# Regrouping the batches of a rope kernel: two single batches at each end, six even pairs between

## The chip, the cores and the metric

The kernel runs on one core of one Trainium2 chip. Times are device microseconds of an execution; the profile's span (first to last instruction) is 1.4 to 1.6 us shorter. Executions fall into a fast and a slow state (before: 161.58 to 161.92 us in five of six runs, 169.21 in one). A run counts as slow when it is over 1.5% above the fastest of the same kernel. Engines are DVE (VectorE), POOL (GpSimd), PE (TensorE), ACT (ScalarE) and SP (SyncE); transfers run on 16 DMA engines (in the packet records of the first profile, of before, 16 or 17 packets are in flight at every half microsecond from 158.0 to 162.5).

## The reference

```python
# x (16, 512, 1024) f32, 16 heads of 64; cos, sin (512, 32)
x = x.reshape(batch, seq, num_heads, 64)
x1, x2 = x[..., :32], x[..., 32:]
rotated = concatenate([x1 * cos - x2 * sin, x1 * sin + x2 * cos], axis=-1)   # f32
```

In and out are 33.55 MB each, and every element is read once and written once.

## The kernel before

A "row" below is one 128 x 1024 piece of work. DVE multiplies it by cos into PSUM (t1), POOL or DVE multiplies the swapped halves by sin into SBUF (t2), and either DVE adds the two, or PE adds t2 onto t1 and ACT copies the sum out. The sum overwrites x in its buffer and is stored from there. A batch alone puts 4 rows on a partition (16 KB packets), a pair of batches 8 rows (32 KB packets); in the packet records of the first profile each transfer has 128 of them.

```python
tiles = [(0, R1)] + [(b, R2) for b in range(1, batch - 1, 2)] + [(batch - 1, R1)]   # R1 = 4, R2 = 8
REGIONS = 5                                              # buffers of 8 rows, used in turn
loads = [(t, r, n) for t, (_, whole) in enumerate(tiles)
         for n in (R1 if t == 1 else whole,) for r in range(0, whole, n)]   # the first pair in two halves
PE2 = [tiles[t][1] == R2 and r in (1, 3, 6) for t, r in rows]    # rows that PE adds
V2 = [tiles[t][1] == R2 and r == V_ROW for t, r in rows]         # rows that DVE multiplies by sin
...
def on_sync(sp):                                         # all loads
    for c, (t, r, n) in enumerate(loads):
        if t >= REGIONS:
            sp.wait_ge(sem_out[t - REGIONS], 16)         # the store that frees the buffer
        sp.dma_start(in_sbuf(t, r, n), in_dram(x1, x2, t, r, n)).then_inc(sem_in[c], 16)
        ...                                              # with the first load, those of cos and sin
...
def on_scalar(ae):                                       # copies of PE's rows, and all stores
    for u in range(NU):
        ...
        if r == tiles[t][1] - 1:
            wait_added(ae, u)
            ae.dma_start(in_dram(o1, o2, t, 0, r + 1), in_sbuf(t, 0, r + 1)).then_inc(...)
...
for u in range(NU + LEAD):                               # DVE; LEAD = 1
    if u < NU: mul(u)                                    # waits for the load of row u
    if u >= LEAD and not PE2[u - LEAD]: comb(u - LEAD)   # the addition of the row before
```

The addition of a transfer's last row comes after the multiply of the next transfer's first row, so a store also waits for the next load.

## Time and profile before

| | before |
|---|---|
| time, median of 6 runs | 161.70 us |
| fast runs | 161.58 to 161.92 us |
| slow run | 169.21 us |
| first profile (slow) | 169.03 us, span 167.5 us |
| POOL, DVE busy in it | 134.2 us, 131.0 us |
| bytes moved | 67.26 MB |

How to read it: POOL and DVE are busy about 80% of a span in which the DMA engines are busy 94%.

### The profile page before, as it was taken

Reading aid. Unit: us, or ns where it says so; the run is one execution under the profiler, and the core shown is the slowest. Engines: PE = TensorE matmul, PEld = TensorE weight load, DVE = VectorE, ACT = ScalarE, POOL = GpSimd, SP = SyncE. Lnnn points to the kernel's source line nnn. Section 1 sums busy time; section 2 is a strip of 40 time slices with the busy share of each in tenths; the row PEclk is TensorE's granted clock in tenths of the full one; section 3 lists DMA queues with packets and bytes.
Section 4 is the critical chain, followed back from the end, with each engine's and each line's share of the span. In section 5 each row is a group of like instructions: output and inputs, shape, how many; then the busy total and the mean of one; then the engine's idle time right before and its main releaser. Section 6 shows DMA issues by size and latency. Waiting matters only on the chain.

```text
span 167.5 us, 565 instructions
## 1 busy us (share of the span) xinstructions
PE 70.2 (42%) x94; PEld 24.2 (14%) x94; DVE 131.0 (78%) x118; ACT 24.0 (14%) x26; POOL 134.2 (80%) x66
## 2 busy tenths in 40 slices
PE   6040039284937672476402907019390392700000
PEld 1020023022211211022101201013020130200000
DVE  0079996999999999999959994398964989999000
ACT  3020002211222040204020222002202022200000
POOL 5069999999999999999949994399954999996000
PEclk9999999855596789558985795855955559675555
DMA  5999999999899999999999999999999999488970
GB/s 160 420 425 431 474 423 387 438 434 446 384 485 384 479 391 470 385 470 407 446 415 430 438 391 477 399 462 407 470 399 419 427 470 415 172 376 376 442 317 23
DMA packets 3026, 67.26 MB, mean 402 GB/s; under 512 B 336, under 2 KB 592, under 8 KB 592
## 3 DMA queue, kind: packets, MB, share of 16 engines
q1 hardware_dynamic: 1728, 33.69, 47.6%
q10 hardware_dynamic: 1296, 33.56, 46.8%
q14 instruction: 2, 0.02, 0.0%
HBM read 33.69 MB, written 33.55 MB: 402 GB/s over the span
## 4 chain that ended last, share of the span: by engine, by line
DMA 48%; DVE 16%; POOL 11%; issue 7%; PE 7%; ACT 2%; SPq 0%; DVEq 0%; POOLq 0%
DMA x_sb<-in_x_dram 25%; DMA out_dram<-x_sb 19%; POOL t_sb L249 11%; DVE t_ps L285 8%; DVE x_sb L296 7%; PE t_ps L206 7%; DMA stage<-in_sin_dram 4%; ACT x_sb L171 2%; DVE t_sb L278 1%; SPq L155 0%; SPq L152 0%; ACT s_sb L161 0%; ACT s_sb L162 0%; POOLq L146 0%; DVEq L295 0%
## 5 line engine op out<-in xcount | busy, mean ns | idle before, releaser
L249 POOL TENSOR_TENSOR t_sb<-x_sb,s_sb 128x1024 f32<-128x1024 f32 x57 | 131.9, 2361 | 18.3 <-DMA x_sb<-in_x_dram 11.7
L206 PE MATMUL t_ps<-t_sb,ident 128*128 128x512 f32 x84 | 65.4, 935 | 68.9 <-POOL t_sb L249 48.6
L285 DVE TENSOR_TENSOR t_ps<-x_sb,pair_ps 128x1024 f32<-128x1024 f32 x56 | 67.5, 1222 | 14.4 <-DMA x_sb<-in_x_dram 11.0
L296 DVE TENSOR_TENSOR x_sb<-t_ps,t_sb 128x1024 f32<-128x1024 f32 x43 | 52.3, 1218 | 0.5 <-POOL t_sb L249 0.5
L206 PEld LDWEIGHTS t_ps<-t_sb,ident 128*128 128x128 f32 x84 | 22.3, 288 | 111.6 <-issue 59.6
L171 ACT ACTIVATE x_sb<-t_ps 128x1024 f32<-128x1024 f32 x21 | 21.5, 1024 | 113.2 <-PE t_ps L206 113.2
L285 DVE TENSOR_TENSOR t_ps<-x_sb,tab_ps 128x1024 f32<-128x1024 f32 x8 | 9.7, 1223 | 0.0
L278 DVE TENSOR_TENSOR t_sb<-x_sb,tab_ps 128x1024 f32<-128x1024 f32 x7 | 8.5, 1215 | 0.0
L256 DVE COPY tab_ps<-stage 128x128 f32<-128x128 f32 x1 | 0.3, 295 | 7.7 <-DMA stage<-in_cos_dram 7.7
L189 PE MATMUL pair_ps<-stage,pick 128*128 128x256 f32 x4 | 2.0, 667 | 5.2 <-DMA stage<-in_sin_dram 5.2
L182 PE MATMUL t_ps<-zero 128*128 128x512 bf16 x6 | 2.7, 630 | 1.3 <-DVE zero L254 1.3
L189 PEld LDWEIGHTS pair_ps<-stage,pick 128*128 128x128 f32 x4 | 1.2, 324 | 6.3 <-issue 6.1
L232 POOL TENSOR_SCALAR_AFFINE_SELECT pick<-pick 128x128 f32<-128x128 f32 x2 | 1.4, 706 | 0.1
L161 ACT ACT_TABLE_LOAD x1 | 1.3, 1283 | 0.8 <-PEq L329 0.8
L161 ACT ACTIVATE s_sb<-stage 128x128 f32<-128x128 f32 x1 | 0.3, 311 | 7.0 <-DMA stage<-in_sin_dram 7.0
L182 PEld LDWEIGHTS t_ps<-zero 128*128 128x128 bf16 x6 | 0.7, 137 | 2.4 <-DVE zero L254 1.2
L254 DVE MEMSET zero<- 128x256 uint32 x1 | 0.3, 272 | 0.9 <-PEq L329 0.9
L165 ACT ACTIVATE s_sb<-pair_ps 128x256 f32<-128x256 f32 x1 | 0.4, 384 | 1.7 <-PE pair_ps L189 1.7
L217 POOL MEMSET ident<- 128x128 f32 x1 | 0.2, 205 | 0.3 <-POOLq L329 0.3
L166 ACT ACTIVATE s_sb<-pair_ps 128x256 f32<-128x256 f32 x1 | 0.4, 377 | 0.0
L219 POOL TENSOR_SCALAR_AFFINE_SELECT ident<-ident 128x128 f32<-128x128 f32 x1 | 0.3, 297 | 0.1
L329 POOL MEMSET const-float32-0.0<- 128x1 f32 x1 | 0.1, 99 | 0.3 <-issue 0.3
(7 smaller groups left out, 1.3 us busy)
## 6 DMA issues: line engine op xcount, KB each, us to landing
out_dram<-x_sb ACTq DMA_DIRECT2D x7, 4096.0 KB, 31.9
x_sb<-in_x_dram SPq DMA_DIRECT2D x6, 4096.0 KB, 42.2
x_sb<-in_x_dram SPq DMA_DIRECT2D x4, 2048.0 KB, 13.8
out_dram<-x_sb ACTq DMA_DIRECT2D x2, 2048.0 KB, 15.8
stage<-in_cos_dram SPq DMA_DIRECT2D x1, 64.0 KB, 7.6
stage<-in_sin_dram SPq DMA_DIRECT2D x1, 64.0 KB, 7.3
```

Source lines behind the costliest of these rows:

```text
L161: ae.activation(s1_sb[:, :, 0, :], sv, COPY, scale=-1.0)
L165: ae.activation(s2[:, :, :, 0, :], pair_ps[:, :, 1, :, :], COPY, scale=-1.0)
L166: ae.activation(s2[:, :, :, 1, :], pair_ps[:, :, 1, :, :], COPY).then_inc(sem_s, 1)
L171: ae.activation(xs[:, k, :], t1_ps[:, u % NT1, :], COPY).then_inc(sem_a, 1)
L182: pe.matmul(t1_ps[:, k, b * BANK:(b + 1) * BANK], zero[:, 0:P], zero[:], start=True, stop=True).then_inc(sem_w, 1)
L189: pe.matmul(pair_ps[:, k].rearrange("p c r d -> p (c r d)"), pick[:, k].rearrange("q s b -> q (s b)"), stage[:].rearrange("q c f -> q (c f)"),
L206: ins = pe.matmul(t1_ps[:, u % NT1, b * BANK:(b + 1) * BANK], ident[:], t2[:, b * BANK:(b + 1) * BANK], start=False, stop=True, skip_group ...
L232: pl.affine_select(out=pick[:, k], in_=pick[:, k], compare_op=mybir.AluOpType.is_equal, fill=0.0, base=-k, pattern=[[-2, P // 2], [0, 2]], ...
L249: pl.tensor_tensor(t2_sb[:, u % NT2, :, :, :], swapped(k), over_heads(s_of(t, r)), mult).then_inc(sem_p, 1)
L278: ve.tensor_tensor(t2_sb[:, u % NT2, :, :, :], swapped(k), over_heads(v_ps), mult)
L285: ve.tensor_tensor(t1_ps[:, u % NT1, :].rearrange("p (h d) -> p h d", d=HALF), x_sb[:, k, :, :, :].rearrange("p h t d -> p (h t) d"), c_of ...
L296: ve.tensor_tensor(xs[:, k, :], t1_ps[:, u % NT1, :], t2_sb[:, u % NT2, :, :, :].rearrange("p h t d -> p (h t d)"), add,).then_inc(sem_v, 1)
```

## The change

Batches 0, 1, 14 and 15 come alone and the twelve between as pairs (2,3) to (12,13). The buffers become one ring of 40 rows with no gap, so 40 rows are loaded up front instead of 36, and a shorter piece is moved at the end: the last pair of before is stored only when all of its 8 rows are done, while batches 14 and 15 are stored one by one. Below, S0 is the transfer of batch 0 alone and P2 that of batches 2 and 3.

```diff
-    tiles = [(0, R1)] + [(b, R2) for b in range(1, batch - 1, 2)] + [(batch - 1, R1)]
-    REGIONS = 5
+    singles = (0, 1, batch - 2, batch - 1)
+    tiles = [(b, R1 if b in singles else R2) for b in range(batch) if b in singles or b % 2 == 0]
+    RING = 5 * R2
...
-    PE2 = [tiles[t][1] == R2 and r in (1, 3, 6) for t, r in rows]
+    PE2 = [R1 <= u < NU - R1 and u % R2 in (1, 3, 6) for u in range(NU)]
...
         def on_sync(sp):
-            for c, (t, r, n) in enumerate(loads):
-                if t >= REGIONS:
-                    sp.wait_ge(sem_out[t - REGIONS], 16)
-                sp.dma_start(in_sbuf(t, r, n), in_dram(x1, x2, t, r, n)).then_inc(sem_in[c], 16)
+            for t, (b, n) in enumerate(tiles):
+                if b * R1 % R2 == 0 and b * R1 >= RING:
+                    k = (b * R1 - RING) // R2
+                    sp.wait_ge(sem_out[k], 16 * stores_of(k))
+                sp.dma_start(in_sbuf(t), in_dram(x1, x2, t)).then_inc(sem_in[t], 16)
...
-                    ae.dma_start(in_dram(o1, o2, t, 0, r + 1), in_sbuf(t, 0, r + 1)).then_inc(
-                        sem_out[t] if t < len(sem_out) else sem_rest, 16
-                    )
+                    k = u // R2
+                    ae.dma_start(in_dram(o1, o2, t), in_sbuf(t)).then_inc(sem_out[k] if k < EARLY else sem_rest, 16)
```

More of the change, by code (lines that the diff above doesn't have):

```diff
@@ L37, in bass_split_heads_rope_kernel @@
     COPY = mybir.ActivationFunctionType.Copy
-    tiles = [(0, R1)] + [(b, R2) for b in range(1, batch - 1, 2)] + [(batch - 1, R1)]
+    singles = (0, 1, batch - 2, batch - 1)
+    tiles = [(b, R1 if b in singles else R2) for b in range(batch) if b in singles or b % 2 == 0]
     NT = len(tiles)
-    REGIONS = 5
+    RING = 5 * R2
     rows = [(t, r) for t, (_, n) in enumerate(tiles) for r in range(n)]
     NU = len(rows)
-    loads = [(t, r, n) for t, (_, whole) in enumerate(tiles) for n in (R1 if t == 1 else whole,) for r in range(0, whole, n)]
-    load_of = [c for c, (_, _, n) in enumerate(loads) for _ in range(n)]
+    EARLY = (NU - RING) // R2
     V_ROW = 3
-    PE2 = [tiles[t][1] == R2 and r in (1, 3, 6) for t, r in rows]
+    PE2 = [R1 <= u < NU - R1 and u % R2 in (1, 3, 6) for u in range(NU)]
     V2 = [tiles[t][1] == R2 and r == V_ROW for t, r in rows]
@@ L68, in bass_split_heads_rope_kernel @@
     with ExitStack() as stack:
-        x_sb = stack.enter_context(nc.sbuf_tensor([P, REGIONS * R2, H, 2, HALF], fp32))
+        x_sb = stack.enter_context(nc.sbuf_tensor([P, RING, H, 2, HALF], fp32))
         t2_sb = stack.enter_context(nc.sbuf_tensor([P, NT2, H, 2, HALF], fp32))
@@ L79, in bass_split_heads_rope_kernel @@
         t1_ps = stack.enter_context(nc.psum_tensor([P, NT1, H * HD], fp32))
-        sem_in = [stack.enter_context(nc.semaphore(f"in{c}")) for c in range(len(loads))]
-        sem_out = [stack.enter_context(nc.semaphore(f"out{t}")) for t in range(NT - REGIONS)]
+        sem_in = [stack.enter_context(nc.semaphore(f"in{t}")) for t in range(NT)]
+        sem_out = [stack.enter_context(nc.semaphore(f"out{k}")) for k in range(EARLY)]
         sem_rest = stack.enter_context(nc.semaphore("rest"))
@@ L111, in bass_split_heads_rope_kernel, with in_dram, in_sbuf @@
         xs = x_sb[:].rearrange("p n h t d -> p n (h t d)")
-        def in_dram(single, pairs, t, r, n):
-            b, whole = tiles[t]
-            cols = slice(r * dim, (r + n) * dim)
-            return single[b, :, cols] if whole == R1 else pairs[:, b:b + 2, cols]
-        def in_sbuf(t, r, n):
-            k = t % REGIONS * R2 + r
+        def in_dram(single, pairs, t):
+            b, n = tiles[t]
+            return single[b] if n == R1 else pairs[:, b:b + 2, :]
+        def in_sbuf(t):
+            b, n = tiles[t]
+            k = b * R1 % RING
             return x_sb[:, k:k + n].rearrange("p n h t d -> p (n h t d)")
@@ L123, in where @@
             t, r = rows[u]
-            return t, r, t % REGIONS * R2 + r
+            return t, r, u % RING
         def swapped(k):
@@ L146, in wait_t2_free, with stores_of @@
                     eng.wait_ge(sem_v, n_comb[v])
+        def stores_of(k):
+            return sum(b * R1 // R2 == k for b, _ in tiles)
         def on_sync(sp):
-            for c, (t, r, n) in enumerate(loads):
-                if t >= REGIONS:
-                    sp.wait_ge(sem_out[t - REGIONS], 16)
-                sp.dma_start(in_sbuf(t, r, n), in_dram(x1, x2, t, r, n)).then_inc(sem_in[c], 16)
-                if c == 0:
+            for t, (b, n) in enumerate(tiles):
[3 more added lines that the diff above has]
+                sp.dma_start(in_sbuf(t), in_dram(x1, x2, t)).then_inc(sem_in[t], 16)
+                if t == 0:
                     for i, (table, sem) in enumerate(((cos, sem_cos), (sin, sem_sin))):
                         sp.dma_start(stage[:, i, :], table.rearrange("(s r) d -> s (r d)", r=R1)).then_inc(sem, 16)
-            sp.wait_ge(sem_rest, 16 * (NT - len(sem_out)))
+            sp.wait_ge(sem_rest, 16 * sum(stores_of(k) for k in range(EARLY, NU // R2)))
         def on_scalar(ae):
@@ L244, in on_gpsimd @@
                 t, r, k = where(u)
-                if t < 2 and r == 0:
-                    pl.wait_ge(sem_s, t + 1)
-                pl.wait_ge(sem_in[load_of[u]], 16)
+                if (t, r) == (0, 0):
+                    pl.wait_ge(sem_s, 1)
+                if (t, r) == (2, 0):
+                    pl.wait_ge(sem_s, 2)
+                pl.wait_ge(sem_in[t], 16)
                 wait_t2_free(pl, u)
@@ L269, in mul @@
                 t, r, k = where(u)
-                if u == 0 or load_of[u] != load_of[u - 1]:
-                    ve.wait_ge(sem_in[load_of[u]], 16)
-                if (t, r) == (1, 0):
+                if r == 0:
+                    ve.wait_ge(sem_in[t], 16)
+                if (t, r) == (2, 0):
                     pair_tables()
```

## The prediction

> **What bounds the kernel now.** I read the page's busy totals first. Two engines, DVE and POOL, look nearly full, which invites the guess that compute is the bound:
>
> ```profile
> PE 70.2 (42%) x94; PEld 24.2 (14%) x94; DVE 131.0 (78%) x118; ACT 24.0 (14%) x26; POOL 134.2 (80%) x66
> ...
> DMA  5999999999899999999999999999999999488970
> GB/s 160 420 425 431 474 423 387 438 434 446 384 485 384 479 391 470 385 470 407 446 415 430 438 391 477 399 462 407 470 399 419 427 470 415 172 376 376 442 317 23
> ...
> q1 hardware_dynamic: 1728, 33.69, 47.6%
> q10 hardware_dynamic: 1296, 33.56, 46.8%
> ```
>
> Row 2 of the page (the 40 slices) contradicts that guess: the DMA row is at 9 in every slice from the second on but for a dent near the end. The queue table says the same in one sum: loads hold 47.6% and stores 46.8% of sixteen engines' span, together 94.4% of 167.5 us = 158.1 us of transfer per DMA engine. Only 9.4 us of the span has no packet on the average engine. So I looked for where those lie, in the table of stretches (columns: us, then PE, PEld, DVE, ACT, POOL busy, clock, DMA share, GB/s):
>
> ```profile
> 140.00:142.00 2.00, 0.00 (x0) 0.00 (x0) 2.00 (x2) 0.11 (x1) 2.00 (x2) 0.89 1.16 500
> 142.00:144.00 2.00, 1.84 (x2) 0.84 (x3) 2.00 (x3) 0.00 (x0) 2.00 (x1) 0.50 0.76 328
> 144.00:146.00 2.00, 1.53 (x3) 0.34 (x1) 2.00 (x3) 0.43 (x1) 2.00 (x2) 0.75 0.08 33
> 146.00:148.00 2.00, 0.00 (x0) 0.00 (x0) 2.00 (x3) 0.59 (x1) 2.00 (x2) 1.00 0.46 197
> ...
> 162.00:164.00 2.00, 0.00 (x0) 0.00 (x0) 0.00 (x0) 0.00 (x0) 0.00 (x0) 0.50 0.25 107
> 164.00:166.00 2.00, 0.00 (x0) 0.00 (x0) 0.00 (x0) 0.00 (x0) 0.00 (x0) 0.50 0.08 33
> ```
>
> The unused time is about 2 us at the start, some 3 us at 144 to 148, and the last 4 us, where a trickle of 33 GB/s is about one engine of sixteen. To see why, I read POOL's timeline:
>
> ```profile
> 86.11 16.22 POOL L249 TENSOR_TENSOR t_sb<-x_sb,s_sb 128x1024 f32<-128x1024 f32 x7 [2.44 <-DMA x_sb<-in_x_dram]
> 107.43 16.22 POOL L249 TENSOR_TENSOR t_sb<-x_sb,s_sb 128x1024 f32<-128x1024 f32 x7 [5.11 <-DMA x_sb<-in_x_dram]
> 127.83 9.30 POOL L249 TENSOR_TENSOR t_sb<-x_sb,s_sb 128x1024 f32<-128x1024 f32 x4 [4.17 <-DMA x_sb<-in_x_dram]
> ```
>
> POOL waits 11.7 us for loads. The sixteen increments of each load's semaphore show what it waited for: the loads needed at 107.4 and 127.8 had landed on fifteen engines by 103.1 and 122.5, and one straggling engine came at 107.36 and 127.76. Its store packets took 1.3 to 1.85 us between 51 and 135 us, against 1.22 elsewhere. So **this profile is of a slow run**: it took 169.03 us, like the one slow run of 169.21, while the other two took 161.58 and 161.66. The verdict is about fast runs, so I first take the straggler out. The profiled run is 1.5 us longer than its span, so a fast span is about 160.1.
>
> **The fast run, rebuilt.** A transfer has 128 packets, 8 to each engine: 32 KB for a pair, 16 KB for a single (and for the halves of the first pair's load). In the packet records a 32 KB packet takes 1.213 us (load) or about 1.22 (store), a 16 KB packet 0.611. Where both queues have work they alternate packet by packet, so 8 rounds of pair against pair last 8 x 2.43 = 19.5 us, pair against single 8 x 1.83 = 14.6, a pair alone 9.7 and a single alone 4.9. The trace agrees: on fifteen engines the pair loads land at 63.6, 83.0, 102.3 and 121.7, 19.4 apart, and the first store (single against pairs) runs from 24 to 39.
>
> On those fifteen engines the last load lands at 136.2 and the store of batches 11 and 12 at 145.4. Without the straggler the last pair's load releases its work at 121.7 instead of 127.8; its store was issued 146.7 - 127.8 = 18.9 later, so now at 140.6, before 145.4: the dent closes. Then 145.4 + 9.7 + 4.9 = **160.0**, against 160.1 expected. So in fast runs the DMA engines have no hole from the first packet to the last, and the end is start (1.9) + all bytes + landing.
>
> [...]
>
> **The change part by part.**
> - Bytes are the same. Per engine, loads stay four 16 KB sets and six 32 KB sets: 32 x 0.611 + 48 x 1.213 = 77.8 us. Stores go from two and seven sets to four and six: 9.8 + 68.3 = 78.1 becomes 19.6 + 58.6 = 78.1. Sum 155.9 either way: **0.0 us**.
> - Start: the first pair's two half loads become two whole singles, 2 MB each as before, so rows 0 to 7 arrive no later. The third load becomes 4 MB where it was the second half, 2 MB; it lands near 24, while POOL gets to row 8 at 9.7 + 8 x 2.36 = 28.6. Hidden.
> - Batch 1 is stored alone, near 30 instead of waiting with batch 2 until 38.2. This only fills the store queue earlier (the trace has it empty at 38 to 42); loads fill the engines then.
> - The ring takes 40 rows up front instead of 36, and the tenth batch waits for two stores (S0 and S1).
> - Matmul additions stay 21. Multiplies on DVE go from 7 to 6 (-1.2 us), POOL's from 57 to 58 (+2.3 us). POOL must finish no later than about 154, and has near 10 us of waiting and tail to give in this trace. Off the path.
> - Tail: pair 12/13, then S14 and S15 alone. Both singles' loads, at 16 KB packets against 32 KB stores, get a third of the engines.
>
> Walk, where DMA is always full (issue to first packet was 1.5 to 3.7 us in the trace):
>
> ```
> us             load           store (issued)
> 1.9 - 23.5     S0, S1, P2     -
> 24 - 38.6      P4             S0 (20.5)
> 38.6 - 53.2    P6             S1 (~30)
> 53.2 - 72.7    P8             P2 (~47)
> 72.7 - 92.1    P10            P4 (~64)
> 92.1 - 111.6   P12            P6 (~80)
> 111.6 - 126.2  S14            P8 (~96)
> 126.2 - 140.8  S15            P10 (~114)
> 140.8 - 150.5  -              P12 (~131)
> 150.5 - 155.4  -              S14 (~144)
> 155.4 - 160.3  -              S15 (~152)
> ```
>
> Every load is issued in time: P10 needs both first stores (53.9) and its turn is 72.7; P12 needs P2's store (73) and its turn is 92.1; S14 needs P4's (92.5) and its turn is 111.6. The critical place is the end. The last addition of a row comes after the next row's multiply, so S14's store waits for S15's load at 141.3. S15 then needs the 10.6 us that the last single took here (144.06 to the issue at 154.7): issue at 151.9, first packet 153.4 to 155.6, its turn 155.4. The margin is about 1 us, where the kernel before has 155.1 - 148.6 = 6.5. A miss of 0 to 0.5 us is likely, no more.
>
> Span 160.3, plus 1.5 = **161.8 us**.
>
> **The rivals.**
> 1. *The finer tail pays.* Reading 144 to 148 at face value, one would say that splitting the last pair fills the hole and gains 3 us (158.6, faster). For it: the hole is real in this profile. Against it: it follows from the straggler, which itself goes on without a hole to 167, so even a slow run is bound by that one engine.
> 2. *The last load comes too late.* If the singles' loads get less than a third, or S15's work is slower than 10.6 us, the store queue runs dry near 155 and all of the lateness shows: 3 us late makes 164.8, slower. For it: the margin of 1 us. Against it: the alternation was exact everywhere in this trace.
> 3. *POOL becomes the bound*, with 58 rows: 9.7 + 58 x 2.33 = 144.8, plus additions and a single's store of 6 us = 153. Hidden even then.
>
> **Range and chances.** The sum says 161.8; fast runs repeat to 0.1 us. Below 161 would need faster packets. Above, rival 2 and a median that falls among slow runs (167 to 169, which I expect for the changed kernel too) pull: range 161.0 to 163.6. Faster by over 2% (below 158.4) needs the DMA floor of 155.9 + 1.9 to fall, 0.03. Slower by over 2% needs over 3 us of dry queue, 0.09. Within 2%: 0.88.
>
> **What would show it.** Right: the DMA row at 9 to the end in a fast profile, two queues near 78 us per engine, P8 onward landing at the walk's times, S15's load as the last wait of POOL and DVE near 141. Wrong in the tail: a dent in DMA share at 152 to 156 with the last single's store issued after it. Wrong in the packets: a mean other than 1.22 or 0.61 us, or a share other than a third for singles. A large fast-run gain would mean that fast runs do have a hole that a slow profile cannot show me.

What the text uses of transfers reads as follows in the packet records and landings of the first profile:

- A 32 KB packet took 1.22 us in the mean, which is 26.9 GB/s on one engine and 430 on sixteen, the rate in the expectations.
- The alternation: between 60 and 80 us 133 load and 128 store packets of 32 KB start. Taken pair by pair, the distances of their starts (60 to 100 us) have their peak at 2.4 to 2.5 us from load to load (586 pairs, against 106 at 1.2 to 1.3) and at 1.2 to 1.3 us from load to a later store (631). With 16 KB stores against 32 KB loads it was less exact: 118 and 96 packets at 24 to 36 us.
- The straggler: the last store has fifteen landings at 162.95 to 163.11 us and one at 167.43; sixteen packets are in flight at 162.5, and one at every half microsecond from 163.0 to 167.0.
- From issue to first packet, where the store queue was empty, it was 3.5 us (20.45 to 23.96) and 4.2 (38.17 to 42.40) with loads running beside it, and 1.2 (146.71 to 147.92, on fifteen engines) without them. The walk has 1.5 to 3.7.

## The result, and the profile after

| | before | after |
|---|---|---|
| median of 6 runs | 161.70 us | 161.35 us |
| fast runs | 161.58 to 161.92 | 161.31 to 161.35 |
| slow runs among the 6 | 169.21 | 164.85, 167.47 |

The ratio is 0.9977 (95% interval 0.9963 to 0.9992): **the same** at the 2% that counts, though 0.2% faster beyond noise. A ratio here is the mean time of one kernel's fast runs over that of the other's of the same rounds, so it is not quite the ratio of the medians.

The first profile after fell in the slow state too (span 166.1 us), and its DMA row has a dent in the third slice from the end, where the kernel before had one in the sixth:

```profile
DMA  5999999999999999999989999999999999999293
```

In each of these two slow profiles one DMA engine fell behind the other fifteen: the last load landed on it 6.3 us after the fifteenth before (143.21 against 136.96) and 5.2 us after it here (146.63 against 141.40). They explain nothing about fast runs. So both kernels were run again for fast profiles (runs before_again and after_again below); all that follows reads those. First the pages, busy times, the DMA row in 40 slices, and the queues; the kernel before, span 160.3 us:

```profile
PE 67.8 (42%) x94; PEld 23.5 (15%) x94; DVE 130.9 (82%) x118; ACT 24.0 (15%) x26; POOL 134.2 (84%) x66
...
DMA  5999999999999999999999999999998999999996
...
q1 hardware_dynamic: 1728, 33.69, 49.7%
q10 hardware_dynamic: 1296, 33.56, 48.6%
```

The changed kernel, span 160.0 us:

```profile
PE 71.4 (45%) x94; PEld 24.0 (15%) x94; DVE 130.3 (81%) x117; ACT 24.0 (15%) x26; POOL 136.5 (85%) x67
...
DMA  5999999999999999999999999999999999999896
...
q1 hardware_dynamic: 1728, 33.69, 49.8%
q10 hardware_dynamic: 1440, 33.56, 48.8%
```

Both DMA rows are full from the second slice to the end: the dent that the slow profile of before had is gone without any change of the kernel. The queue lines give the rest. Before, 49.7% + 48.6% = 98.3% of 160.3 us is 157.6 us of transfer on the average DMA engine; after, 49.8% + 48.8% = 98.6% of 160.0 us is 157.8 us. The work of the DMA engines is the same to 0.2 us, and 2.7 and 2.2 us of the span are left over, some 2.1 of them in the first 4 us, before all engines are running (the packet records of the two first profiles have 2.1 and 2.0 there).

Next, POOL's timeline in the same two runs (start, length, what, and in brackets the wait before it). Before:

```profile
83.79 16.23 POOL L249 TENSOR_TENSOR t_sb<-x_sb,s_sb 128x1024 f32<-128x1024 f32 x7 [0.20 <-DMA x_sb<-in_x_dram]
103.11 16.23 POOL L249 TENSOR_TENSOR t_sb<-x_sb,s_sb 128x1024 f32<-128x1024 f32 x7 [3.09 <-DMA x_sb<-in_x_dram]
122.48 25.45 POOL L249 TENSOR_TENSOR t_sb<-x_sb,s_sb 128x1024 f32<-128x1024 f32 x11 [3.14 <-DMA x_sb<-in_x_dram]
```

After:

```profile
9.52 99.41 POOL L254 TENSOR_TENSOR t_sb<-x_sb,s_sb 128x1024 f32<-128x1024 f32 x43 [6.45 <-ACT s_sb L166]
111.57 25.46 POOL L254 TENSOR_TENSOR t_sb<-x_sb,s_sb 128x1024 f32<-128x1024 f32 x11 [2.64 <-DMA x_sb<-in_x_dram]
140.65 9.27 POOL L254 TENSOR_TENSOR t_sb<-x_sb,s_sb 128x1024 f32<-128x1024 f32 x4 [3.62 <-DMA x_sb<-in_x_dram]
```

Both wait for loads over 6 us in all, POOL's own work went up by one multiply, and the end did not care. The 3.62 us before S15's rows is the wait that the prediction's walk placed at 141.3; it ended at 140.65.

Last the end of the span by stretches of 2 us (the columns are those of the prediction's second fence). Packets at a border push one stretch below 1 and its neighbour above; only a low share with no excess beside it is a hole. Before:

```profile
146.00:148.00 2.00, 0.00 (x0) 0.00 (x0) 2.00 (x3) 0.00 (x0) 1.93 (x1) 0.50 1.14 492
148.00:150.00 2.00, 0.00 (x0) 0.00 (x0) 1.69 (x2) 0.00 (x0) 0.00 (x0) 0.50 0.72 311
150.00:152.00 2.00, 0.00 (x0) 0.00 (x0) 0.00 (x0) 0.00 (x0) 0.00 (x0) 0.50 1.14 492
152.00:154.00 2.00, 0.00 (x0) 0.00 (x0) 0.00 (x0) 0.00 (x0) 0.00 (x0) 0.50 0.95 410
154.00:156.00 2.00, 0.00 (x0) 0.00 (x0) 0.00 (x0) 0.00 (x0) 0.00 (x0) 0.50 0.90 385
```

After:

```profile
148.00:150.00 2.00, 0.00 (x0) 0.00 (x0) 0.94 (x1) 0.00 (x0) 1.92 (x1) 0.50 0.79 336
150.00:152.00 2.00, 0.00 (x0) 0.00 (x0) 1.23 (x1) 0.00 (x0) 0.00 (x0) 0.50 0.99 426
152.00:154.00 2.00, 0.00 (x0) 0.00 (x0) 0.00 (x0) 0.00 (x0) 0.00 (x0) 0.50 1.09 467
154.00:156.00 2.00, 0.00 (x0) 0.00 (x0) 0.00 (x0) 0.00 (x0) 0.00 (x0) 0.50 0.96 410
156.00:158.00 2.00, 0.00 (x0) 0.00 (x0) 0.00 (x0) 0.00 (x0) 0.00 (x0) 0.50 0.95 410
```

DVE and POOL are done before 150 in the one and before 152 in the other, and the DMA engines go on without a hole: their last packets end between 158.6 and 159.9 us before, and between 158.6 and 159.5 us after.

### The profile page after: what moved, and what is told of

It reads as the page before. It is cut to its first block, busy times and chain, and to the rows that moved or that the text cites. A ratio compares the mean times of both kernels' runs of the same rounds, so it can differ in the third digit from the quotient of the medians.

```text
span 166.1 us, 568 instructions
## 1 busy us (share of the span) xinstructions
PE 72.6 (44%) x94; PEld 24.6 (15%) x94; DVE 130.5 (79%) x117; ACT 24.0 (14%) x26; POOL 136.6 (82%) x67
## 2 busy tenths in 40 slices
DMA packets 3170, 67.26 MB, mean 405 GB/s; under 512 B 352, under 2 KB 608, under 8 KB 608
## 4 chain that ended last, share of the span: by engine, by line
DMA 52%; POOL 15%; issue 11%; DVE 8%; PE 6%; ACT 1%; SPq 1%; POOLq 0%; DVEq 0%; ACTq 0%
DMA x_sb<-in_x_dram 33%; DMA out_dram<-x_sb 19%; POOL t_sb L254 15%; PE t_ps L209 6%; DVE x_sb L301 4%; DVE t_ps L290 4%; ACT x_sb L175 1%; SPq L156 1%; SPq L159 1%; DVE t_sb L283 0%; DVEq L300 0%; POOLq L145 0%; POOLq L143 0%; ACTq L136 0%
## 5 line engine op out<-in xcount | busy, mean ns | idle before, releaser
L254 POOL TENSOR_TENSOR t_sb<-x_sb,s_sb 128x1024 f32<-128x1024 f32 x58 | 134.2, 2355 | 18.7 <-DMA x_sb<-in_x_dram 11.7
L209 PE MATMUL t_ps<-t_sb,ident 128*128 128x512 f32 x84 | 67.8, 966 | 65.3 <-POOL t_sb L254 45.1
L290 DVE TENSOR_TENSOR t_ps<-x_sb,pair_ps 128x1024 f32<-128x1024 f32 x48 | 57.9, 1222 | 8.1 <-DMA x_sb<-in_x_dram 4.8
L290 DVE TENSOR_TENSOR t_ps<-x_sb,tab_ps 128x1024 f32<-128x1024 f32 x16 | 19.3, 1222 | 7.1 <-DMA x_sb<-in_x_dram 6.7
L283 DVE TENSOR_TENSOR t_sb<-x_sb,tab_ps 128x1024 f32<-128x1024 f32 x6 | 7.3, 1215 | 0.0
```

Source lines behind the costliest of these rows:

```text
L209: ins = pe.matmul(t1_ps[:, u % NT1, b * BANK:(b + 1) * BANK], ident[:], t2[:, b * BANK:(b + 1) * BANK], start=False, stop=True, skip_group ...
L254: pl.tensor_tensor(t2_sb[:, u % NT2, :, :, :], swapped(k), over_heads(s_of(t, r)), mult).then_inc(sem_p, 1)
L283: ve.tensor_tensor(t2_sb[:, u % NT2, :, :, :], swapped(k), over_heads(v_ps), mult)
L290: ve.tensor_tensor(t1_ps[:, u % NT1, :].rearrange("p (h d) -> p h d", d=HALF), x_sb[:, k, :, :, :].rearrange("p h t d -> p (h t) d"), c_of ...
```

## The experiments

"Before" in a group is the kernel before on the same chip in the same rounds. Every kernel that computes the whole result was correct.

**Fast profiles of the two kernels, unchanged.** A first single run of before took 170.49 us, slow by its time. It is the third slow profile with one lagging engine: its last load landed there at 144.67 us, on the fifteenth at 136.19.

> The kernel before, unchanged, for a profile of a fast run, which the first profile was not. Theory: no hole in the DMA row from 4 us on: the store of batches 13 and 14 is issued near 140.6, before its turn at 145.4, DMA ends near 159.2, span 160.1. Rival 1: the dent of 3 us at 144 to 148 is there in a fast run too.

> The kernel before, unchanged, once more for a profile of a fast run. Theory: time 161.7; the DMA row has no dent between 4 us and the last packet, idle time of the average DMA engine 2.1 us at the start and 0.7 at the end (as in the fast profiles of the other kernels), POOL's waits for loads near 2 and 3 us as the walk has it. Rival 1: a dent near 144 to 148 in a fast run.

> The changed kernel, unchanged, for a profile of a fast run. Theory: 161.35; no dent; S15's load lands near 140.3 and its store is issued near 151.2 and waits for its turn at 154.9 less the latency. Rival 2: the last store's first packet comes after 155 with a dent before it.

before_again: 161.42, 161.82 and 162.28 us in fast runs (ratio to before 1.0003), one slow of 165.43; the profile is a fast one of 161.82. The store of batches 11 and 12 landed at 145.7 on its last engine, that of 13 and 14 at 155.4, the last at 160.2; the rebuilt run of the prediction had 145.4, 155.1 and 160.0. after_again: six fast runs, median 161.47, ratio 0.9979 (0.9967 to 0.9991), which repeats the first result. So rival 1's hole is an effect of the slow state, and is in neither of the two fast profiles.

**Do the engines that compute matter? (a_halfwork)**

```diff
-  pl.tensor_tensor(t2_sb[:, u % NT2, :, :, :], swapped(k), over_heads(s_of(t, r)), mult)
+  h = H if u < R2 else H // 2
+  pl.tensor_tensor(t2_sb[:, u % NT2, 0:h, :, :], swapped(k)[:, 0:h], over_heads(s_of(t, r))[:, 0:h], mult)
   # and the same for DVE's two multiplies and its addition; the result is wrong on purpose
```

> The changed kernel, with POOL's and DVE's multiplies and additions on half of the heads from row 8 on (result wrong on purpose, all transfers the same). Theory: POOL and DVE fall from about 135 to about 80 us busy and the time stays at 161.3, within 0.4. Rivals 2 and 3 (the last load's lateness, or POOL, sets the end): well below 161, for POOL as the bound by tens of us, for the last row's lateness by some us.

161.30 us, ratio to before 0.9973, so the same as the changed kernel (0.9977), in five fast runs. Its page:

```profile
PE 58.6 (37%) x94; PEld 21.9 (14%) x94; DVE 78.8 (49%) x117; ACT 24.0 (15%) x26; POOL 82.5 (52%) x67
...
DMA  5999999999999999999999999999999999999996
```

POOL fell from 136.5 to 82.5 us busy and DVE from 130.3 to 78.8, and nothing of it reached the time: rivals 2 and 3 are out at this size, and compute is not the bound.

**Fewer bytes, the same compute (a_lessload)**

```diff
+  if b == 10:
+      sp.dma_start(xs[:, k, :], x2[:, b:b + 2, 0:dim]).then_inc(sem_in[t], 16)   # one row of eight
+  else:
       sp.dma_start(in_sbuf(t), in_dram(x1, x2, t)).then_inc(sem_in[t], 16)
```

> The changed kernel, loading one row of eight of batches 10 and 11 (result wrong on purpose, same work on the engines): 3.67 MB less, 8.5 us at 430 GB/s. Theory: the time falls until compute is next. Transfers alone would end at 161.3 - 8.5 = 152.8; POOL without any load wait ends at 10.0 + 58 x 2.33 = 145.2, last addition 146.6, last store first packet near 148.4, 4.9 us of it and 0.9 to land: span 154.2, time 155.7. So about 155.7. Rival 3 (compute is the bound already): no change, 161.3.

The 0.9 us to land here, and 0.7 in a_pairtail, are estimates; in the first profile after, the last data packet ended 0.35 us before the last landing (165.67, 166.02).

155.47 to 156.95 us, median 156.6. Taking 3.67 MB away gave 4.8 us of the 8.5 that these bytes take, 5.9 in the fastest run, which is the profiled one. In it all of POOL's 58 multiplies ran in one stretch with no wait:

```profile
9.66 134.30 POOL L258 TENSOR_TENSOR t_sb<-x_sb,s_sb 128x1024 f32<-128x1024 f32 x58 [6.58 <-ACT s_sb L170]
```

That invites the reading that POOL was the next bound, as expected. The end of the span says otherwise:

```profile
148.00:150.00 2.00, 0.00 (x0) 0.00 (x0) 0.00 (x0) 0.00 (x0) 0.00 (x0) 0.50 1.04 442
150.00:152.00 2.00, 0.00 (x0) 0.00 (x0) 0.00 (x0) 0.00 (x0) 0.00 (x0) 0.50 0.67 287
152.00:154.00 2.00, 0.00 (x0) 0.00 (x0) 0.00 (x0) 0.00 (x0) 0.00 (x0) 0.50 0.17 74
```

Compute was done at 145.3 and the last store issued at 145.4. On ten DMA engines its shares landed together at 151.5 to 151.6; on the other six they landed at 152.7 to 154.0, because these engines lagged and were still at the store before (landed there at 147.9 to 149.2). So lagging engines set the end of this run. The ten give an estimate of where compute alone would end: 151.6, which with the 1.5 us from the last landing to the time makes 153.1 us, some 8 us below the changed kernel. The other three runs (156.4 to 157.0) have no profile. The DMA engines bound the kernel, and the two experiments show it from both sides: less compute gains nothing, fewer bytes gain 5 us.

**How much room has the last store? (a_late5, a_late2, b_late5, b_late3)** The addition of the last row is repeated, which changes no result and delays the last store by about 1.25 us for each repeat (five took 6.25 us in the trace of b_late5; the expectations count 1.24).

```diff
   def comb(u):
+      for i in range(5 if u == NU - 1 else 0):          # 2, 3 or 5
+          ve.tensor_tensor(xs[:, k, :], t1_ps[...], t2_sb[...], add).then_inc(sem_late, 1)
+          ve.wait_ge(sem_late, i + 1)
       ve.tensor_tensor(xs[:, k, :], t1_ps[...], t2_sb[...], add).then_inc(sem_v, 1)
```

> The changed kernel, with the last row's addition done six times in sequence instead of once: the last store is issued 5 x 1.24 = 6.2 us later. Theory (the last store waits for its turn in the DMA engines, margin 1 us by my walk, up to 3 if the last load lands 1.5 to 2 us sooner as fifteen engines of the profile show): 161.35 + 6.2 - margin = 164.5 to 166.6. If the end of compute set the end (no margin): 167.5. If the margin were as large as in the kernel before: 162 to 163.

> The changed kernel, with the last addition done three times: 2.5 us later. With six it rose by 4.0 of 6.2 us. Theory (a margin of 2.2 us, then a slope of one): 161.35 + 0.3 = 161.65, at most 161.9. If every lateness shows in part (a slope of 0.65 from the start): 162.95.

Five repeats on the changed kernel: 165.35 us, so 4.0 of 6.2 us showed and 2.2 were absorbed. Two repeats: 161.67 us, so 0.2 to 0.3 of 2.5 us showed. Both give a margin of 2.2 us, after which lateness shows in full: from two repeats to five the delay grew by 3.7 us and the time by 3.7. The stretches of a_late5 show what a dry store queue looks like:

```profile
152.00:154.00 2.00, 0.00 (x0) 0.00 (x0) 1.93 (x3) 0.00 (x0) 0.00 (x0) 0.50 0.86 369
154.00:156.00 2.00, 0.00 (x0) 0.00 (x0) 1.97 (x2) 0.00 (x0) 0.00 (x0) 0.50 0.02 8
156.00:158.00 2.00, 0.00 (x0) 0.00 (x0) 1.58 (x2) 0.00 (x0) 0.00 (x0) 0.50 0.00 0
158.00:160.00 2.00, 0.00 (x0) 0.00 (x0) 0.00 (x0) 0.00 (x0) 0.00 (x0) 0.50 0.93 393
```

From 154 to 158 hardly a packet starts, while DVE is at its repeats. In this trace the last store was issued at 157.7 and its first packet started at 158.55, 0.85 us later. In after_again the issue is at 151.3 and the first packet starts at 153.9: it waited 1.7 us for its turn on the first engine, and up to some 2.5 on the last.

> The kernel before, with the last row's addition done six times in sequence: the last store is issued 6.2 us later. In the changed kernel this cost 4.0 us, so its margin is 2.2. Here the theory has the last store issued at 148.6, first packet 1.5 to 1.7 us later, turn at 155.1: margin 4.8 to 5.0, so the time rises by 1.2 to 1.4 us, to 163.0. If both kernels had the same margin: 165.7.

> The kernel before, with the last addition done four times: 3.7 us later. The first try with six gave 164.7 to 165.9, but in its profile three DMA engines lagged by some 4 us, which alone ends at the same time. Theory (margin 4.8 to 5.0 without a lagging engine): the fastest runs stay at 161.6 to 161.9. If the margin is that of the changed kernel, 2.2: 163.2.

Five repeats on the kernel before: 164.71, 165.50 and 165.88 us in runs called fast (and a slow one of 168.79), more than the 163.0 expected. The profile, of the 165.88 run, has three DMA engines that lag. The last load landed at 140.1, where it landed at 137.2 in the fast profile of before, and the last store was issued at 157.8, 8.0 us later than there (149.8) instead of 6.2. The last landing came 4.1 us later (164.29 against 160.22), so 3.9 were absorbed. Three repeats: 161.38 to 163.35 us, median 162.07, ratio 1.002 (0.9984 to 1.0056): no cost that can be told from noise, the best runs at 161.4 to 161.7 as expected. Its profile, of the 162.23 run, has the issue 4.5 us later (154.3) and the last landing 0.4 later (160.63): 4.1 absorbed. So the margin of the kernel before is about 4 us, from one profile each, not the 4.8 to 5.0 of the expectation. The fast trace of before agrees: its last store is issued at 149.8, not 148.6, and its turn comes at 153.8 to 155.0, by engine; less 0.85 us from issue to first packet, as in a_late5, that leaves 3.1 to 4.4.

**One end of the change at a time (b_splittail, a_pairtail, b_splithead)**

```diff
   # b_splittail: before, the store of the last pair in two halves of 4 rows (b_splithead: of the first pair)
-  if r == tiles[t][1] - 1:
+  n = R1 if t == NT - 2 else tiles[t][1]                # b_splithead: t == 1
+  if r % n == n - 1:
   # a_pairtail: after, batches 14 and 15 as a pair again
-  singles = (0, 1, batch - 2, batch - 1)
+  singles = (0, 1)
```

> The kernel before, with the store of its last pair (batches 13 and 14) cut into two 2 MB stores, the first issued after row 4 of 8: the tail part of the change alone. Theory (the DMA engines have no hole in a fast run, so a finer tail has nothing to fill): 161.7 us, within 0.3 of the kernel before. Rival 1 (the hole of 3 us at 144 to 148 is real in fast runs): about 158.6. If the 0.35 us that the change did gain comes from the tail, 161.35.

161.76 to 162.02 us in fast runs, ratio 1.0008 (0.9993 to 1.0023): the finer tail alone gains nothing, as the theory had it and rival 1 had not. (Two runs were slow, one of 168.37 us and one of 301.95; for the second see the end.)

> The changed kernel, with batches 14 and 15 as a pair again: the start of the change alone. Theory: the pair's load lands near 130.5 (half share from 111), its last row is done some 19 us later, its store of 4 MB has its first packet at 151, against a turn of 150.0; then 9.7 us and 0.7 to land: span 161.4 to 162.4, time 162.9 to 163.8, so that the single tail is needed in this layout and gains 1.5 to 2.5 us against it, though nothing against the kernel before. Rival (the end never waits for compute): 161.35.

162.31 to 162.93 us in three fast runs, ratio 1.0108 (1.0048 to 1.0168), and a slow one of 164.93. The end of the span of the fastest:

```profile
146.00:148.00 2.00, 0.00 (x0) 0.00 (x0) 2.00 (x3) 0.00 (x0) 0.86 (x1) 0.50 0.80 344
148.00:150.00 2.00, 0.00 (x0) 0.00 (x0) 1.15 (x2) 0.00 (x0) 0.00 (x0) 0.50 0.50 213
150.00:152.00 2.00, 0.00 (x0) 0.00 (x0) 0.00 (x0) 0.00 (x0) 0.00 (x0) 0.50 1.23 524
152.00:154.00 2.00, 0.00 (x0) 0.00 (x0) 0.00 (x0) 0.00 (x0) 0.00 (x0) 0.50 0.61 262
```

P12's last packets end between 148.8 and 149.9. P14's store could be issued only when all of its 8 rows were done, at 149.24, and its first packets start together at 150.45: a hole of about 1 us, as expected. (The swing from 1.23 to 0.61 is no hole: the engines now run in step, and a packet is booked where it starts.) The three times lie at or below the lower end of the expected 162.9 to 163.8. So the new start needs the new tail; against a pair at the end the single tail gains 1.0 to 1.6 us, and against the old kernel nothing, since that had a single at its end as well.

> The kernel before, with the store of its first pair (batches 1 and 2) cut into two 2 MB stores, the first issued 9 us sooner: it fills the store queue, which is empty at 38 to 42. Theory (the engines are full of loads there): 161.7, same as before. If the change's 0.35 us come from stores that begin sooner: 161.35.

161.49 to 161.70 us, ratio 0.9985 (0.9973 to 0.9997), six fast runs of six. Storing half of the first pair sooner is perhaps a part of the change's 0.2%, and a finer tail alone is not; the interval is too wide to say more. This run also moves the end of compute without altering the tail: its last load landed at 130.9 instead of 137.2 and its last store was issued at 143.3 instead of 149.8. Being 6.5 us earlier moved the time by 0.15%. In the fast traces the shares of the last store land between 158.96 and 160.22 us before, and between 158.96 and 159.92 after: the last of the sixteen engines ends 0.3 us sooner. What makes it do so stays open.

## Why the prediction was right or wrong

It was right: 161.35 us against 161.8, inside 161.0 to 163.6, and the same within 2%.

- **The bound.** The step "in fast runs the DMA engines have no hole from the first packet to the last" was argued from a slow profile with one lagging engine taken out. The fast profile of before shows it, and a_halfwork and a_lessload show it by experiment. The three landings that it rebuilt were right to 0.3 us. One reading in the rebuilding was off: it released the last pair's work at 121.7, while its own lines have the fifteen engines done at 122.5. So the store that it put at 140.6 was issued at 141.7 in the fast profile, still before its turn.
- **The bytes.** Loads 77.8 and stores 78.1 us per engine, either way, were to make no difference: the queue lines give 157.6 and 157.8 us. Both are near 1.8 us above the sum of 155.9, alike in the two kernels: 1.3 us are load packets that took longer than 0.611 and 1.213, by the packet records of after_again, and 0.6 us packets of 512 bytes and less, by those of the first profile after.
- **The walk.** Read in after_again as the last share of each store: S1 52.98 (walk 53.2), P2 72.98 (72.7), P4 92.35 (92.1), P6 111.7 (111.6), P8 126.3 (126.2), P10 140.8 (140.8), P12 150.3 (150.5), S14 155.1 (155.4), S15 159.9 (160.3). Every turn came within 0.4 us of where it was put. The 0.4 us of excess at the end lies in the three stores that run alone there: 19.15 us (140.77 to 159.92) for the walk's 19.5. The last single load landed at 140.6, 0.7 before its mark. The alternation was less exact than the prediction says: the first store had 5.8 of 16 engines at 24 to 36 us by the packet records of the first profile, where strict turns give 16 x 0.611 / 1.83 = 5.3.
- **The tail margin.** "About 1 us" was too small and the "6.5" of the kernel before too large; measured, 2.2 and about 4. The first used 1.5 us or more from issue to first packet, where the last store took 0.85 with its queue empty (a_late5; 0.84 on fifteen engines of the first profile after, 157.38 to 158.22), and put the turn at 155.4, where the first packets start at 153.9 to 154.7. The second left this latency out and put the issue at 148.6, 1.2 too early. None of these errors reached the time, because the last store waited for its turn all the same. The direction held: the change made the tail tighter, not looser, and it is still not the end.
- **The rivals.** The finer tail (1) fell with b_splittail and the fast profile of before. Rival 2's mechanism is real, as a_late5 shows beyond 2.2 us, but its size was not reached. POOL (3) fell with a_halfwork, and the trace of a_lessload puts the end of compute about 8 us below.
- **The slow state.** It was expected at 167 to 169 us for the changed kernel too; 167.47 and 164.85 came. "Fast runs repeat to 0.1 us" was too narrow: those of the kernel before run from 161.42 to 162.28.

## What to carry to other kernels

Before a hole in a profile is taken as something to fill, check the state of the run that it was taken in: here 3 us of idle DMA in a slow profile were one engine's lateness, and neither fast profile had them. Here the bytes at the measured packet times already gave 155.9 of 160 us, and regrouping the transfers moved the time by 0.2%; in such a case ask instead how many microseconds the last store can be late before the queue runs dry, and measure it by delaying that store on purpose. Here a few microseconds of added work at the end told the margin, which no share of busy time did. And a profile called fast can still have lagging engines: look at when each of a transfer's sixteen shares lands before you name the next bound.

## What else the runs showed

- The rate: with one core at work, loads and stores mixed, the fast run before_again moved 420 GB/s over the whole span (67.26 MB in 160.3 us). Even the first, slow profile moved 428 from 2 to 142 us.
- The shares of two queues: with 16 KB packets on the store queue and 32 KB on the load queue, 94 store and 97 load packets started at 39 to 50 us of the first profile after, and the stores held 5.2 of the 16 engines, a third. The store of S1 took 14.5 us in after_again (38.4 to 53.0); S15, with nothing beside it, took 4.8 (155.1 to 159.9).
- An engine that lags in some executions only. In the slow profile of before the last share of a store landed 7 us behind the fifteenth (107.53 against 100.66 us) with that engine's packets at 1.3 to 1.85 us for 1.22. It comes in degrees: the last load landed late on one engine by 5 to 9 us in the three slow profiles, on three by some 3 us in b_late5 and on six by 1 to 4 us in a_lessload, both called fast. The traces do not tell which engine it is. Of the timed runs of the kernel before 13 of 44 were slow, and 3 of 16 of the altered ones with its start (b_splittail with its 301.95, b_late5, b_late3); of the kernels that store batch 1, or half of the first pair, early, 3 of 41. The cause is open.
- One run of b_splittail took 301.95 us with the granted clock recorded as 1.0 throughout, while a matmul took 3026 ns, against 905 in the fast run of before, and a POOL multiply 2353 ns, against 2355. What slowed the matmuls is not shown:

```profile
L207 PE MATMUL t_ps<-t_sb,ident 128*128 128x512 f32 x84 | 230.3, 3026 | 39.6 <-DVE t_ps L286 30.9 <-POOL t_sb L250 8.7
```
